# A gated pooling and matrix-memory block on one core: row mathematics in turns, folded mixer maps, pooled columns gated and split in the input projection, matrix memory's rows loaded four chunks ahead

## The chip, the cores and the metric

The kernel runs on one core of a Trainium2 chip. The metric is the device time of one launch in microseconds, lower is better. A core has five engines that work side by side and meet through semaphores: TensorE (PE; its weight loads are listed as PEld), VectorE (DVE), ScalarE (ACT), GpSimd (POOL) and SyncE (SP), which in this kernel issues all DMA transfers from one queue.

## The reference, cut to what matters

The input is 2048 tokens of 1024 columns, float32. One projection makes all columns for two branches that are merged at the end:

```python
h = rms_norm(x, norm_pre_g)
u_a, z_a, q, k, v, o, z_b, gates, g_a, g_b = split(h @ w_in)

pooled = multiscale_pool(u_a)          # 4 groups of 256 columns, centred means over 2, 4, 8, 16 tokens, minus the token
mixed  = einsum('bsgc,gcd->bsgd', pooled, pool_mix_w)          # one 256 x 256 map for each group
y_a    = (mixed * pool_scale) * silu(z_a)

q, k = silu(centred_depthwise_conv(q, k))                      # 5 taps
h_fwd = mlstm_direction(q, k, v, i_pre[0], f_pre[0])           # 4 heads of 256, 16 chunks of 128 tokens
h_bwd = flip(mlstm_direction(flip(q), flip(k), flip(v), ...))
y_b = rms_norm_per_head(h_fwd + h_bwd) * mlstm_norm_g * sigmoid(o) * silu(z_b)

merged = sigmoid(g_a + b0) * (y_a @ w_proj_pool) + sigmoid(g_b + b1) * (y_b @ w_proj_mlstm)
out = x + rms_norm(merged @ w_out, norm_post_g)
```

In each direction of the matrix memory, a chunk adds its weighted keys and values to a 256 x 256 state, and its queries read the state and the other tokens of the chunk. The weights come from "row mathematics": for every direction, head and chunk, sums of the logarithms of the forget gates, running maxima, and exponentials of both.

## The kernel before

All products are made from float32 values split into a high and a low part ("hi" and "lo", type float32r): three matmuls (hi x hi, hi x lo, lo x hi) take the place of one (`mm3`, `acc3`). `split` makes the parts: ScalarE copies the high part, and VectorE or GpSimd subtracts it from the value. The state and score products of the matrix memory are plain float32.

**Input projection** (`phase1`). The tokens are done in two halves of 1024. The columns are done in 36 pairs of 128-column blocks (`in_pairs`). The first two pairs of each half are plain products (`quarters`). Each other pair is a Strassen product of seven parts, 12 matmuls of 128 x 128 by 512 each, in three pairs of PSUM banks A, B and C (`strassen`). `prep_w` makes the weight combinations in the first half and `keep_w` stores them to memory; in the second half `again_w` reads them back. The columns of a pair are finished by a function of its kind: `pair_qk` (convolution and SiLU), `pair_v` (transposes), `pair_u` (window sums, pooled columns to memory), `pair_z` (SiLU), `pair_o` and `pair_g` (gates). The function is a generator: its last part runs while the next pair's products are under way (`run(rest)`). Long tiles come from small pools with rotating buffers: "raw" three, "acc" four, "p" six, and one buffer "rb" in the pool `rows`.

With half 1, `row_math` does the row mathematics of all gates in the place before pair 6 in one piece (L515), with two round trips through memory ("ends", "carry"). `masked` then adds the triangular masks to the rows of each two chunks and stores them ("nm"), and the convolutions left over from the first half (`late_load`) use the "rb" buffer afterwards.

**Matrix memory** (`tail`, `mlstm`). For each head, `backward` makes the states of the backward direction one chunk at a time (`back0` loads keys and values, `back1` transposes and weighs keys, `back2` updates the state), sixteen chunks ahead of `front1` to `front3`, which do both directions of a chunk: scores, decay, the products, the forward state, the division. `load_rows` reads the masked rows (tile "negM", from "nm") and the scale rows ("isc") of two chunks, two chunks ahead. `finish` makes the output of four chunks and puts its store in a list that is issued after the step (L1310).

**Branch A** (`branch_a`) does the pooling branch's projection for 8 blocks of 256 tokens. `mixer` comes two blocks ahead of it: it loads pooled columns and SiLU gates, splits the pooled columns, multiplies them by the group's map (`mix_weights`, 48 matmuls in a block), applies scale and gate, and splits the result for `project`. **Branch B** (`branch_b`) projects the matrix memory's output and merges. **Output** (`output`) is a Strassen product again, with the norm and the residual.

The order of the instructions on each engine is made by the compiler's scheduler from the order of the program, with priorities (`high_priority`) and ties (`issue_after`) written in it.

Of the kernel before, what the change touches and what calls it, by code (L numbers as in the profile page):

```python
# [8 lines left out]
F32 = mybir.dt.float32  # L9
# [4 lines left out]
P = 128  # L14
# [23 lines left out]
LAP = 1  # L38
PB = 2
# [3 lines left out]
PX = "kT"  # L43
# [4 lines left out]
def in_pairs():  # L48
# [11 lines left out]
    light = [("v", 0), ("o", 0), ("z", 0), ("o", 1), ("v", 1), ("o", 2), ("z", 1), ("o", 3), ("v", 2), ("o", 4)]  # L60
    light += [("z", 2), ("o", 5), ("v", 3), ("o", 6), ("z", 3), ("o", 7)]
# [16 lines left out]
class Kernel:  # L78
# [21 lines left out]
    def mm3(self, ps, w, x, start, stop):  # L100

        nc = self.nc
        for kt in range(4):
# [4 lines left out]
            nc.tensor.matmul(ps, wl, xh, start=False, stop=stop and kt == 3, skip_group_check=True)  # L108


    def constants(self):
        nc, a = self.nc, self.a
        c = self.ctx.enter_context(self.tc.tile_pool(name="const", bufs=1))
        self.cpool = c
        load = self.load
        self.gpre = load("norm_pre_g", [P, KT])
        self.ident = load("ident", [P, P])
        self.halo_qk = c.tile([P, 16, 4], F32, tag="halo_qk", name="halo_qk")
        self.halo_u = c.tile([P, 8, 16], F32, tag="halo_u", name="halo_u")
        self.half_c = c.tile([P, 1], F32, tag="half_c", name="half_c")  # L120
# [4 lines left out]
        self.icnt = {}  # L125
        for w in WINDOWS:
# [10 lines left out]
    def load(self, name, shape):  # L137
        t = self.cpool.tile(shape, F32, tag=name, name=name)
        self.nc.sync.dma_start(t, self.a[name])
        return t  # L140
# [72 lines left out]
    def operands(self, half, H, hp, wc, pool, psum):  # L213
# [47 lines left out]
        if half == 0:  # L261
            with tc.high_priority():
                last = sums(0)
            self.cw = self.load("conv_w", [P, 16, TAPS])
            self.cb = self.load("conv_b", [P, 16])
            self.bm = self.load("b_merge", [P, 2, KT])
# [37 lines left out]
    def load_w(self, wr, i, kts):  # L304
        raw = wr.tile([P, 4, 2 * P], F32, tag="wraw", name=self.nm("wraw"))
        self.nc.sync.dma_start(raw, self.a["w_in"][i, :, kts, :])
        return raw

    def again_w(self, W, i, wr, wc):

        nc, w_in = self.nc, self.a["w_in"]
# [9 lines left out]
        nc.sync.dma_start(left, w_in[i, :, :, :P])  # L321
# [11 lines left out]
        self.read = nc.sync.dma_start(b22, w_in[i, :, 4:8, P:])  # L333
# [35 lines left out]
    def strassen(self, H, W, psum, pool, out, n=BLK, swap=False):  # L369
# [13 lines left out]
        def prod(k, h, w, start):  # L383
            x, y = (H[h], W[w]) if not swap else (W[w], H[h])
            self.mm3(bank[k], y, x, start, True)
# [12 lines left out]
        prod("B", "S3", "T3", False)  # L398
# [38 lines left out]
    def phase1(self):  # L437
        tc, nc, a = self.tc, self.nc, self.a
        with ExitStack() as es:
            hp = {  # L440
# [18 lines left out]
            wg = None  # L459
            n = len(self.pairs)  # L460
            late, waits = [(kind, h) for h in range(NH) for kind in "qk"], None
            for half in range(2):
# [49 lines left out]
                rest = iter(())  # L512
# [1059 lines left out]
```

## Time and profile before

| what | us |
|---|---|
| median of 3 runs | 2386.11 |
| lowest and highest | 2384.36, 2393.65 |
| the profiled execution | 2388.18 |
| its span, first to last instruction | 2386.4 |
| mean granted TensorE clock | 0.993 of full |

The stages follow each other in the span. By TensorE's work: the first half of the input projection until about 739 us, the second until about 1456, the matrix memory until about 1790, branch A until about 2031, branch B until about 2213, then the output.

The span is one execution on the chip as the hardware profiler recorded it. A line of groups gives source line, engine, operation, tiles written and read, shape, count, then busy time and mean duration in ns, and then the idle time of the engine ahead of these instructions with what ended it. A tile view gives shortest, median and longest duration, and the start of the first and the last instruction. A windows view gives, for each stretch, its length and then busy time and instruction count of each engine, the granted clock and the DMA load. The chain of waits is followed back from the last instruction, so a transfer or an engine in it is what the rest stood for. Matmuls are pipelined: durations of neighbours overlap, and a busy share says less than how many start in a microsecond.

### The profile page before, as it was taken

To read this page: it belongs to the slowest core of one execution; us is meant where nothing else is said; L and a number is where in the kernel's file an instruction comes from. 1 tells how busy PE (TensorE), PEld (TensorE's weight loads), DVE (VectorE), ACT (ScalarE), POOL (GpSimd) and SP (SyncE) were. 2 spreads that over 40 slices of the span, in tenths; PEclk is the share of its full clock that TensorE was granted. 3 is DMA by queue.
4 is the path that set the end of the run, shared out by engine and by line. 5 is a ranking of instruction groups with operands and counts; after the bars stand their busy time and mean duration, and the time that the engine had idled before them with its cause. 6 is when DMAs were issued, how large, how long until landed. Compare 5 with 4: busy or idle time off the path is not lost.

```text
span 2386.4 us, 35771 instructions
## 1 busy us (share of the span) xinstructions
PE 2313.3 (97%) x12569; PEld 1998.1 (84%) x12569; DVE 1468.2 (62%) x2495; ACT 898.2 (38%) x1773; POOL 1139.3 (48%) x902
## 2 busy tenths in 40 slices
PE   7899999999999989999999999998999999999998
PEld 5688888888887878888888887997989899999776
DVE  6876676677666465565666434887875333354765
ACT  5435333333334333323322234766764112120442
POOL 4655564555544434464564540554555111233775
PEclk9999999999999999999999999999999999999999
DMA  4467656566673566787787867766657546588763
GB/s 151 175 225 273 234 194 238 203 230 215 233 260 135 166 192 216 260 282 256 246 272 239 269 221 253 231 214 208 197 161 230 176 146 208 183 283 280 249 215 124
DMA packets 303011, 521.63 MB, mean 219 GB/s; under 512 B 27504, under 2 KB 138224, under 8 KB 302832
## 3 DMA queue, kind: packets, MB, share of 16 engines
q1 hardware_dynamic: 302832, 519.35, 65.3%
q8 instruction: 99, 1.62, 0.3%
q14 instruction: 80, 0.66, 0.1%
HBM read 318.45 MB, written 200.80 MB: 218 GB/s over the span
## 4 chain that ended last, share of the span: by engine, by line
PE 79%; DVE 8%; DMA 7%; issue 2%; POOL 2%; ACT 2%; SPq 1%; DVEq 0%; POOLq 0%; ACTq 0%
PE bankB L106 8%; PE bankB L107 8%; PE bankB L108 8%; PE bankA L108 5%; PE bankA L107 5%; PE bankC L107 5%; PE bankA L106 5%; PE bankC L106 5%; PE bankC L108 5%; PE num L1212 3%; PE pb L921 2%; PE pb L922 2%; PE pb L920 2%; PE paps L921 2%; PE paps L922 2%
## 5 line engine op out<-in xcount | busy, mean ns | idle before, releaser
L98 POOL TENSOR_TENSOR wB21l<-wraw,wB21h 128x512 fp32r<-128x512 f32 x76 | 107.6, 1416 | 218.9 <-ACT wB21h L94 178.8
L627 DVE SCALAR_TENSOR_TENSOR acc<-raw,conv_w,acc 128x1026 f32<-128x1026 f32 (+1 forms) x96 | 155.8, 1636 | 10.6 <-ACT acc L622 9.7
L1196 POOL TENSOR_TENSOR qs<-q,isc 128x256 f32<-128x256 f32 x120 | 91.6, 766 | 145.3 <-PE num L1212 63.4
L98 POOL TENSOR_TENSOR wB22l<-wraw,wB22h 128x512 fp32r<-128x512 f32 x76 | 116.6, 1535 | 77.8 <-ACT wB22h L94 55.8
L922 PE MATMUL pb<-oxs,w_proj_mlstml 128*128 128x256 f32 x512 | 143.8, 281 | 0.0
L921 PE MATMUL pb<-oxs,w_proj_mlstmh 128*128 128x256 f32 x512 | 143.8, 281 | 0.0
L920 PE MATMUL pb<-oxs,w_proj_mlstmh 128*128 128x256 f32 x512 | 143.5, 280 | 0.0
L921 PE MATMUL paps<-pys,w_proj_poolh 128*128 128x256 f32 x512 | 142.6, 281 | 0.2 <-POOL pys L98 0.2
L920 PE MATMUL paps<-pys,w_proj_poolh 128*128 128x256 f32 x512 | 141.6, 281 | 1.2 <-DVE sga L1049 1.2
L922 PE MATMUL paps<-pys,w_proj_pooll 128*128 128x256 f32 x512 | 141.3, 281 | 0.0
L98 POOL TENSOR_TENSOR wB11l<-wraw,wB11h 128x512 fp32r<-128x512 f32 x72 | 108.9, 1513 | 54.4 <-ACT wB11h L94 53.6
L395 DVE TENSOR_TENSOR u<-bankB,p 128x512 f32<-128x512 f32 x76 | 52.2, 687 | 107.8 <-PE bankB L108 95.1
L106 PE MATMUL bankC<-S1h,wT1h 128*128 128x512 f32 x272 | 106.5, 392 | 3.4 <-ACT sg L738 3.4
L106 PE MATMUL bankB<-S3h,wT3h 128*128 128x512 f32 x272 | 106.3, 391 | 2.3 <-DVE u L395 2.3
L108 PE MATMUL bankB<-S2h,wT2l 128*128 128x512 f32 x272 | 106.3, 391 | 1.2 <-DVE wT2l L98 1.2
L106 PE MATMUL bankA<-A12h,wB21h 128*128 128x512 f32 x272 | 106.8, 393 | 0.5 <-ACT p L389 0.5
L107 PE MATMUL bankB<-S2l,wT2h 128*128 128x512 f32 x272 | 107.0, 393 | 0.0
L106 PE MATMUL bankB<-A22h,wT4h 128*128 128x512 f32 x272 | 105.9, 389 | 0.8 <-DVE u L400 0.8
L108 PE MATMUL bankC<-S1h,wT1l 128*128 128x512 f32 x272 | 106.5, 392 | 0.0
L107 PE MATMUL bankC<-S1l,wT1h 128*128 128x512 f32 x272 | 106.4, 391 | 0.0
L106 PE MATMUL bankB<-S2h,wT2h 128*128 128x512 f32 x272 | 106.2, 391 | 0.0
L107 PE MATMUL bankB<-S3l,wT3h 128*128 128x512 f32 x272 | 106.0, 390 | 0.0
(443 smaller groups left out, 7677.9 us busy)
## 6 DMA issues: line engine op xcount, KB each, us to landing
wraw<-in_w_in SPq DMA_DIRECT2D x110, 512.0 KB, 4.4
wt<-wT2h SPq DMA_DIRECT2D x34, 256.0 KB, 3.8
wt<-wT1h SPq DMA_DIRECT2D x34, 256.0 KB, 4.6
wt<-wT3h SPq DMA_DIRECT2D x34, 256.0 KB, 3.8
wt<-wT2l SPq DMA_DIRECT2D x34, 256.0 KB, 4.8
wt<-wT1l SPq DMA_DIRECT2D x34, 256.0 KB, 4.3
wt<-wT3l SPq DMA_DIRECT2D x34, 256.0 KB, 3.1
wt<-wT4h SPq DMA_DIRECT2D x34, 256.0 KB, 2.0
```

The source lines that it names most:

```text
L98: return eng.tensor_tensor(lo, x, hi.bitcast(F32), op=ALU.subtract)
L106: nc.tensor.matmul(ps, wh, xh, start=start and kt == 0, stop=False, skip_group_check=True)
L107: nc.tensor.matmul(ps, wh, xl, start=False, stop=False, skip_group_check=True)
L108: nc.tensor.matmul(ps, wl, xh, start=False, stop=stop and kt == 3, skip_group_check=True)
L395: self.read_banks.append(nc.vector.tensor_tensor(u2, bank["B"], p1, op=ALU.add))
L627: nc.vector.scalar_tensor_tensor(acc[:, :n], raw[:, tap : tap + n], self.cw[:, ct, tap : tap + 1], acc[:, :n], op0=ALU.mult, op1=ALU.add,)
L920: nc.tensor.matmul(ps, wh, xh, start=i == 0, stop=False)
L921: nc.tensor.matmul(ps, wh, xl, start=False, stop=False)
L922: nc.tensor.matmul(ps, wl, xh, start=False, stop=i == n)
L1196: nc.gpsimd.tensor_tensor(qs[d], q[:, :, ck], isc[:, d, j % 2, None, :].to_broadcast([P, 2, P]), op=ALU.mult)
L1212: nc.tensor.matmul(pn, qs[d][:, kt, :], state[:, kt, :], start=kt == 0, stop=False)
```

## The change

- **Row mathematics in turns.** `row_math` becomes a generator with six parts, one each in the places of pairs 3, 4, 6, 7, 9 and 10 of the second half. Each part but the last ends after it has issued DMAs whose results the next part reads. The leftover convolutions begin at pair 10 in place of 7.
- **Mixer's maps folded.** Pooling works on tokens and the map on columns, so the map can be applied to the input weights first. A new generator `fold` multiplies each group's 1024 x 256 block of `w_in` by its map times the scale, in float32, and stores it ("wu"). It runs in eight steps in the first half, with a load part in the place of one pair and a product part in that of the next. The pairs "u" read these weights.
- **Pooled columns gated and split in the input projection.** `pair_u` reads the SiLU gates of its columns, multiplies, splits, and stores both parts ("ya"). The pairs "z" move ahead of the "u" of the same group. `mixer` and `mix_weights` are gone; `pooled` in their place loads the two parts. The weight tiles of branch A that are loaded inside the matrix memory are more by the rooms that the maps took.
- **Matrix memory's rows loaded four chunks ahead**, with three buffers in place of two for the masked rows. Keys are read one chunk earlier than values, and gates in the fourth chunk of a group in place of the second.
- Tiles that only the projection needs go to a pool `first`, which is given back after it.

```diff
+FOLDS = (3, 5, 7, 9, 12, 14, 16, 18)
+ROWS = (3, 4, 6, 7, 9, 10)
...
+    def fold(self, pool, psum):
+        nc, a, tc = self.nc, self.a, self.tc
+        for g in range(4):
+            for half in range(2):
+                room = self.rows.tile([P, HALF], F32, tag="rb", name=self.nm("fm"))
+                m, sc = room[:, : 2 * DH].rearrange("p (c n) -> p c n", c=2), room[:, 2 * DH : 3 * DH]
+                nc.sync.dma_start(m, a["pool_mix_w"][g])
+                nc.sync.dma_start(sc, a["pool_scale"][g * DH : (g + 1) * DH].partition_broadcast(P))
+                w = pool.tile([P, 2, 4 * P], F32, tag="acc", name=self.nm("fw"))
+                nc.sync.dma_start(w, a["w_uT"][g, :, :, half * 4 * P : (half + 1) * 4 * P])
+                yield
+                nc.gpsimd.tensor_tensor(m, m, sc[:, None, :].to_broadcast([P, 2, DH]), op=ALU.mult)
+                for k2 in range(2):
+                    ps = psum.tile([P, 2, DH], F32, tag="tr", name=self.nm("fps"), bufs=2)
+                    for k in range(2):
+                        n0 = (k2 * 2 + k) * P
+                        with tc.issue_after(self.third.ins):
+                            for ct in range(2):
+                                nc.tensor.matmul(
+                                    ps[:, k, :], w[:, ct, n0 : n0 + P], m[:, ct, :], start=ct == 0, stop=ct == 1
+                                )
+                    o = pool.tile([P, 2, DH], F32, tag="p", name=self.nm("fo"))
+                    nc.scalar.activation(o, ps, AF.Copy)
+                    kt = half * 4 + k2 * 2
+                    nc.sync.dma_start(self.sp[f"wu{g}"][:, kt : kt + 2, :], o)
+                yield
...
-                    if half == 1 and i == 6:
-                        self.row_math(psum)
+                    if half == 1 and i in ROWS:
+                        with tc.issue_after(self.read.ins):
+                            next(rowmath, None)
...
-            nc.sync.dma_start(self.sp[f"pooled{g}"][:, i, tstart : tstart + n], d[:, :n])
+            z = pool.tile([P, HALF + 24], F32, tag="acc", name=self.nm("zu"))
+            nc.sync.dma_start(z[:, :n], self.sp[f"zs{g}"][:, i, tstart : tstart + n])
+            nc.vector.tensor_tensor(d[:, :n], d[:, :n], z[:, :n], op=ALU.mult)
+            nc.scalar.activation(z[:, :n].bitcast(F32R), d[:, :n], AF.Copy)
+            nc.gpsimd.tensor_tensor(d[:, :n].bitcast(F32R), d[:, :n], z[:, :n], op=ALU.subtract)
+            for p, y in enumerate((z, d)):
+                nc.sync.dma_start(self.sp[f"ya{g}"][:, p, i, tstart : tstart + n], y[:, :n])
...
-    def mixer(self, t, mix, ya):
+    def pooled(self, t, ya):
         for g in range(4):
             ys = ya[t, g] = self.pair_of("v1h" if g < 2 else "v1l", "pys")
+            for p in range(2):
+                self.nc.sync.dma_start(ys[:, p].bitcast(F32), self.sp[f"ya{g}"][:, p, :, t * TT : (t + 1) * TT])
...
-                nm = io.tile([P, 2, 2, P], F32, tag="negM", name=self.nm("negM"), bufs=SB)
+                nm = io.tile([P, 2, 2, P], F32, tag="negM", name=self.nm("negM"), bufs=SI)
...
-                if j % 2 == 0 and at + 2 < NH * NC_:
-                    load_rows((at + 2) // NC_, (at + 2) % NC_)
-                if j == 1:
+                if j % 2 == 0 and at + 4 < NH * NC_:
+                    load_rows((at + 4) // NC_, (at + 4) % NC_)
+                if j == 3:
                     load_gates(h, g)
...
             def aside():
-                mix.extend(self.mix_weights(raws, w1))
-                WA.update(self.weights("w_proj_pool", 0, range(2), raws, w1))
+                WA.update(self.weights("w_proj_pool", 0, range(6), raws, w1))
...
-            self.mixer(1, mix, ya)
-            WA.update(self.weights("w_proj_pool", 0, range(6, 8), raws, w2))
-            WA.update(self.weights("w_proj_pool", 1, range(8), raws, w2))
+            self.pooled(1, ya)
+            WA.update(self.weights("w_proj_pool", 1, range(2, 8), raws, w2))
```

More of the change, by code (lines that the diff above doesn't have):

```diff
@@ L125, in constants @@
         self.icnt = {}
+        c = self.first
         for w in WINDOWS:
@@ L135, in constants, with load @@
             self.icnt[w] = (lo, hi)
-    def load(self, name, shape):
-        t = self.cpool.tile(shape, F32, tag=name, name=name)
+    def load(self, name, shape, pool=None):
+        t = (pool or self.cpool).tile(shape, F32, tag=name, name=name)
         self.nc.sync.dma_start(t, self.a[name])
@@ L439, in phase1 @@
         with ExitStack() as es:
+            self.first = es.enter_context(tc.tile_pool(name="first", bufs=1, side="right"))
+            self.constants()
             hp = {
@@ L511, in phase1 @@
                 run(ops)
[L512 removed]
+                rest, fold = iter(()), self.fold(pool, psum)
                 for i in range(2, n):
[L514 to L515 removed]
+                    if half == 1 and i == 8:
                         mask = self.decay.tile([P, 2, P], F32, tag="mask", name="mask", bufs=1)
@@ L540, in phase1 @@
                     run(rest)
+                    if half == 0 and i in FOLDS:
+                        next(fold)
                     next(this)
                     rest = this
+                    if half == 0 and i + 1 in FOLDS:
+                        next(fold)
                     if half == 1 and waits is not None and i >= 7 and self.pairs[i][0] not in "qkuv":
@@ L546, in phase1 @@
                         waits = None
-                    elif half == 1 and waits is None and late and i >= 7:
+                    elif half == 1 and waits is None and late and i >= 10:
                         with tc.issue_after(self.read.ins):
@@ L770, in spills @@
                 sp[f"v{p}{h}"] = self.dram(f"v{p}{h}", [P, NC_, DH + 2])
-            for k in ("pooled", "zs", "sga", "sgb"):
+            sp[f"wu{h}"] = self.dram(f"wu{h}", [P, KT, 2 * P])
+            sp[f"ya{h}"] = self.dram(f"ya{h}", [P, 2, 2, S])
+            for k in ("zs", "sga", "sgb"):
                 sp[f"{k}{h}"] = self.dram(f"{k}{h}", [P, 2, S])
@@ L968, in out_weights @@
             self.split(*o, made[n], "act", "pool" if k % 2 else "dve")
-    def mix_weights(self, raws, pool):
-        nc = self.nc
-        out = []
-        for g in range(4):
-            raw = raws.tile([P, 2, DH], F32, tag="wraw", name=self.nm("mraw"))
-            nc.sync.dma_start(raw, self.a["pool_mix_w"][g])
-            out.append(tuple(pool.tile([P, 2, DH], F32R, tag="w", name=self.nm(f"mx{p}")) for p in "hl"))
-            self.split(*out[g], raw, "act", "dve")
-        return out
     def wt(self, W, kt, n0, n=P):
@@ L1052, in branch_a @@
                 if d == 1 and t + 2 < n:
-                    self.mixer(t + 2, mix, ya)
+                    self.pooled(t + 2, ya)
     def mlstm(self, aside=None, then=None, last=None):
```

119 lines of the change are left out of this document (58 added, 61 removed).

## The prediction

> **What bounds the kernel now.** I read the page first: the busy shares and the shares of the chain that ended last.
>
> ```profile
> PE 2313.3 (97%) x12569; PEld 1998.1 (84%) x12569; DVE 1468.2 (62%) x2495; ACT 898.2 (38%) x1773; POOL 1139.3 (48%) x902
> PE 79%; DVE 8%; DMA 7%; issue 2%; POOL 2%; ACT 2%; SPq 1%; DVEq 0%; POOLq 0%; ACTq 0%
> ```
>
> TensorE sets the time, and the 21% of the chain that is not TensorE shows where it runs dry. "Busy" hides part of that, because the matmuls overlap. So I counted instructions by stretch: the count after the second number (TensorE's) against that of a full neighbour.
>
> ```profile
> core 0: us, PE busy (x) PEld busy (x) DVE busy (x) ACT busy (x) POOL busy (x), PEclk, DMA share, GB/s
> 480.00:540.00 60.00, 59.81 (x272) 49.45 (x271) 46.28 (x57) 20.34 (x35) 33.17 (x23) 1.00 0.67 234
> 840.00:870.00 30.00, 23.67 (x105) 19.11 (x104) 12.09 (x35) 7.44 (x13) 7.08 (x6) 0.94 0.57 125
> 900.00:930.00 30.00, 30.00 (x135) 24.82 (x134) 8.71 (x16) 7.24 (x12) 5.18 (x4) 1.00 0.71 240
> 1500.00:1560.00 60.00, 60.00 (x429) 56.99 (x428) 54.50 (x182) 42.12 (x127) 30.66 (x41) 1.00 0.67 208
> 1600.00:1650.00 50.00, 41.37 (x262) 37.24 (x260) 36.16 (x122) 31.49 (x90) 21.05 (x27) 0.93 0.74 234
> 1740.00:1790.00 50.00, 44.27 (x277) 40.19 (x276) 37.58 (x131) 31.75 (x92) 28.96 (x36) 0.97 0.60 175
> ```
>
> At 840 to 870, 30 of 135 instructions are missing: 30 / 4.5 per us = 6.7 us lost. At 1500 to 1560 the matrix memory runs at 7.15 per us; 1600 to 1650 lacks 358 - 262 = 96, or 13.4 us, and 1740 to 1790 lacks about 80, or 11 us (a rough figure, since the mix of matmuls changes there). The input projection elsewhere is full (480 to 540).
>
> **The change part by part.**
>
> **1. The mixer leaves the tail.** The tile views of its matmuls (first and last of three lines) and of the second branch's projection (likewise):
>
> ```profile
> L920 PE MATMUL mps<-pxs,mxh x128: 276/281/390, 1790.6 to 1985.1; 128*128 128x256 f32 x128
> L922 PE MATMUL mps<-pxs,mxl x128: 276/280/289, 1790.9 to 1985.3; 128*128 128x256 f32 x128
> L920 PE MATMUL pb<-oxs,w_proj_mlstmh x512: 276/280/288, 2031.5 to 2212.5; 128*128 128x256 f32 x171
> L922 PE MATMUL pb<-oxs,w_proj_mlstml x512: 276/281/286, 2031.8 to 2212.8; 128*128 128x256 f32 x171
> ```
>
> The 280 ns are latency, not cost: 3 x 512 matmuls of branch B take 2212.8 - 2031.5 = 181.3 us, 118 ns each. Branch A has as many, and from the first mixer matmul to the first of branch B are 2031.5 - 1790.6 = 240.9. The difference, 59.6 us, is 3 x 128 mixer matmuls x 118 ns = 45.3 and 14.3 of stalls. What ends those stalls stands in the chain:
>
> ```profile
> 1803.59 3.60 DMA xz<-pooled
> ...
> 1824.48 6.51 DMA wraw<-in_w_proj_pool
> ...
> 1860.12 4.65 DMA pa<-sga
> ```
>
> The loads of pooled columns, their splits and the shared buffers go with the mixer; two reads per group and step remain, as many bytes as before and two steps ahead. Late next are the weights: six chunks (second half of the columns) are still loaded when the matrix memory ends, four load rooms are there, and they cover 96 matmuls x 118 ns = 11.3 us. First split, one more load (6.5 us) and the last splits take about as long: a stall between 0 and 8 us, taken as 3. **Term: -59.6 + 3 = -56.6.**
>
> **2. Matrix memory's rows.** The chain in 1600 to 1680, what SyncE's queue issued before the first of these waits, and what that queue itself waited for:
>
> ```profile
> 1603.87 7.39 DMA negM<-nm
> ...
> 1626.55 8.26 DMA negM<-nm
> ...
> 1639.97 2.86 DMA wraw<-in_w_proj_pool
> ...
> 1668.21 9.28 DMA negM<-nm
> ```
> ```profile
> 1600.42 1.94 SPq L1152 DMA_DIRECT2D gb<-gB  x2
> 1602.46 0.66 SPq L1114 DMA_DIRECT2D v<-vl  x1
> ...
> 1603.87 1.57 SPq L1156 DMA_DIRECT2D negM<-nm  x2
> ```
> ```profile
> SPq L1160 <- POOL qs L1196: 49.1, 20, 6.5
> SPq L1156 <- ACT dm L1188: 20.3, 13, 3.9
> ```
>
> ```profile
> L1185 PE MATMUL s<-q,kT x256: 270/275/582, 1486.0 to 1790.5; 128*128 128x128 f32 x128
> ```
>
> The masked rows come behind gates and values in one queue, and wait for one of two buffers. The 64 chunks take 304.5 us by their score products, 4.76 each: four chunks are 19 us instead of 9.5 for two, and a third buffer makes them usable; that covers the 7.4 to 9.3 us. The inter-chunk scale rows keep three buffers, so their place in the queue moves but not the buffer they wait for; behind that wait stand keys, values, queries, gates and the stored results, all needed two chunks later or more. The keys' read one chunk earlier and the gates' two later move no work. I take 8 of the 13.4 us, 1 for the wait at 1668, and 3 of the 11 at the end, where the mixer's splits of its first columns disappear but the splits of four chunks of weights stay: **-12** (bounds 0 and -24).
>
> **3. Row mathematics in turns.** Chain at 840 to 870:
>
> ```profile
> 844.54 9.51 DMA ends<-rows
> 854.12 5.00 DMA rows<-ends
> ...
> 861.66 1.97 PE vtr L653 x8
> ```
>
> VectorE sat behind a row operation that waited for two round trips through memory, with the split of transposed values behind it and TensorE behind that. In turns, each trip has a pair or more (7 products x 12 matmuls x 30 / 135 = 19 us) to land. The operations are the same; constants that move to other memory cost nothing. The late convolutions start three pairs later, and eight slots remain for eight. **-6** (bounds 0, -6.7).
>
> **4. The folds.** Eight steps x 2 x 2 x 2 = 64 products of full float32, 256 columns. The nearest rows are the state products, 258 columns, float32:
>
> ```profile
> 1734.97 0.87 PE num L1212 x4
> ```
> ```profile
> L1212 PE MATMUL num<-cf,qs 128*128 128x258 f32 x240 | 66.1, 385 | 0.0
> ```
>
> 60 chunks x 2 products gave 240 instructions, so each is two, of 0.87 / 4 = 218 ns. 64 x 2 x 218 ns = **+27.8 us**, in a stretch where TensorE is full, so all of it on the path. The GpSimd product ahead of each step and 16 ScalarE copies lie beside it (those engines are 48% and 38% busy), and so do eight times four reads and two stores; were TensorE to wait for the GpSimd product (1.4 us like the splits, by the group below), 8 x 1.4 = 11 more. I take 0: the loads come a whole pair earlier.
>
> **5. Pooled columns gated and split.** Sixteen tiles gain a load, a VectorE product, a ScalarE copy, a GpSimd difference and a second store. The nearest rows of about 1024 elements, and a split:
>
> ```profile
> L684 DVE TENSOR_TENSOR win<-win x24: 1204/1542/2331, 349.5 to 1295.1; 128x1016 f32<-128x1016 f32 x6, 128x1032 f32<-128x1032 f32 x6, 128x1020 f32<-128x1020 f32 x2, 128x1028 f32<-128x1028 f32 x2
> L632 POOL TENSOR_TENSOR acc<-acc,raw 128x1026 f32<-128x1026 f32 x16 | 41.3, 2578 | 16.5 <-ACT raw L631 16.3
> L631 ACT ACTIVATE raw<-acc 128x1026 f32<-128x1026 f32 x16 | 17.0, 1065 | 34.7 <-DVE acc L627 34.7
> L98 POOL TENSOR_TENSOR wT1l<-wt,wT1h 128x512 fp32r<-128x512 f32 x34 | 47.2, 1387 | 93.9 <-ACT wT1h L94 79.9 <-DVE pooled L688 5.4 <-DVE p L704 4.8
> ```
>
> VectorE gets 16 x 1.54 = 25 us, GpSimd 16 x 2.58 = 41, against the 1486 us before the first score product: room on average, not where the windows are widest:
>
> ```profile
> 505.46 2.20 DVE win L684
> ...
> 1286.41 2.69 DMA pooled<-pooled
> 1289.11 1.94 POOL win L684
> ...
> 1300.53 0.50 PE bankB L106
> ```
>
> The chain runs through such tiles at two of the eight groups, near 505 and near 1286. There the next tile's first sum waited for a store to free its buffer, and TensorE for VectorE. The four buffers now serve one tile more, and before its store lie 1.54 + 1.07 + 2.58 = 5.2 us more. The new loads and stores are queued on SyncE ahead of weight reads; what they hold up there is read a pair, 19 us, ahead. A floor is 0 (TensorE's banks hide it; sigmoid columns no longer follow the widest group), a ceiling is four tiles (those of two groups, where the chain leaves TensorE) x (5.2 + 2.7) = 32. I take the products alone, 4 x 1.54 = **+6**, because TensorE at 480 to 540 lost almost nothing with such a chain.
>
> A rule that speaks against this: the Trainium skill, "SBUF — State Buffer", section "Who interferes with whom", says that a VectorE operation with two SBUF inputs and a GpSimd operation that reads SBUF shut each other out for a whole instruction. The spread above (1204 to 2331 ns for one shape class) agrees that such operations are sometimes lengthened, without showing by whom. By the rows alone this part costs 6 us; by that rule it is the third rival below.
>
> **The sum.** -56.6 - 12 - 6 + 27.8 + 6 = -40.8. The profiled run took 2388.18 us (span 2386.4 and 1.8 around it), 2.1 above the median of the three runs; the difference applied to that median, 2386.1, gives **2345 us**.
>
> **The rivals.**
> - **More is recovered:** the matrix memory gets all 24, the pooled tiles hide: -56.6 - 24 - 6.7 + 27.8 = -59.5, 2327 us. For it: every stall named is a wait, not work. Against: VectorE is busy 54.5 of 60 there. 12%.
> - **The rows are a cover:** another load takes their place (weights at 1639.97, the scale rows' 49.1 us of queue waits), and the matrix memory gains nothing: 2357. Against: the masked rows' wait is the longest piece of each gap. 18%.
> - **VectorE and GpSimd in each other's way at the pooled tiles.** The 16 differences hold up VectorE for their length, 2.58 us; at the tiles of the two widest groups of each half, eight, it reaches TensorE, 20.6 us, and half of the 11 at the folds, where a GpSimd product and VectorE's weight differences meet, 5.5: 2371. For it: the spread of 1204 to 2331 ns. Against: VectorE is 62% busy. 14%. (It is what the page of the Trainium skill on SBUF, cited in part 5, would make of this change.)
> - **Slower: the four buffers of the pooled tiles.** If the next window sum waits for the split's store at all 16 tiles, in VectorE's order with evacuations behind it, each costs up to 7.9 us (5.2 + 2.7). Without my 6 the sum is -46.8, so it decides from 46.8 / 16 = 2.9 us per tile that reach TensorE; at half of 7.9 it is 63 - 46.8 = +16, 2402 us. Against: so far only two of eight groups let a chain through. 6%.
> - **No gain at all as described** cannot be for part 1: the matmuls are gone from the stage.
>
> **How the numbers follow.** Forecast 50%, the rivals as given (12, 18, 14, 6). Half a per cent (12 us) is about what a measurement can tell from no change: 2374 and 2398 bound "same". Faster: 50 + 12 + 18 + 6 of the 14 = 86%; same: the other 8; slower 6. The range 2325 to 2373 leaves out the slow case, half of the third and a little at the lower end: under 20%.
>
> **What would show each step.** Right: branch A 182 to 188 us with no mixer matmuls; 128 new matmul instructions of about 218 ns in the first half, which grows by 28 to 36 us; no gap at 840 to 870 and no wait on masked rows in the chain; a matrix memory stage 10 to 15 us shorter. Wrong: TensorE waits on VectorE after each pooled group (part 5); the fold's products waiting for GpSimd (part 4); the first projection of branch A waiting for weights for over 8 us (part 1).

## The result, and the profile after

The changed kernel is slower by half a per cent: a median of 2399.17 us in seven runs, against 2386.11 in seven of the kernel before beside them; the ratio is 1.0054 (95% interval 1.0044 to 1.0064). The forecast was 2345 us, with a range of 2325 to 2373. The profiled execution has a span of 2397.5 us, 11.1 more than before.

The page of the changed kernel, busy shares (its chain of waits reaches back only over the output stage, so the stages are read from tile and windows views):

```profile
PE 2308.5 (96%) x12313; PEld 1986.5 (83%) x12313; DVE 1453.8 (61%) x2411; ACT 881.0 (37%) x1737; POOL 1157.4 (48%) x894
```

TensorE issues 256 matmul instructions fewer (384 of the mixer gone, 128 of the folds new) and yet the span grew. The tile views of the folds, the scores and both branches (columns as before):

```profile
L337 PE MATMUL fps<-fm,fw x128: 377/379/454, 122.4 to 448.9; 128*128 128x256 f32 x128
...
L1221 PE MATMUL s<-q,kT x256: 270/275/582, 1555.4 to 1855.3; 128*128 128x128 f32 x128
...
L978 PE MATMUL paps<-pys,w_proj_poolh x512: 274/281/582, 1839.6 to 2041.1; 128*128 128x256 f32 x171
...
L978 PE MATMUL pb<-oxs,w_proj_mlstmh x512: 274/281/356, 2041.4 to 2222.9; 128*128 128x256 f32 x171
```

From such first and last starts comes a table by stage. "Half 1" ends here with the last product of tile A11h with B11h in the second half's first pair (758.8 before, 805.3 after), "half 2" with the first score, "matrix memory" with the last score, "branch A" with the first projection of branch B. The first of these ends, in the kernel before and in the changed one:

```profile
L426 PE MATMUL bankA<-A11h,wB11h x8: 389/390/393, 739.6 to 758.8; 128*128 128x512 f32 x8
```
```profile
L463 PE MATMUL bankA<-A11h,wB11h x8: 389/389/389, 786.2 to 805.3; 128*128 128x512 f32 x8
```

| us | before | after | difference |
|---|---|---|---|
| half 1 | 758.8 | 805.3 | +46.5 |
| half 2 | 727.2 | 750.1 | +22.9 |
| matrix memory | 304.5 | 299.9 | -4.6 |
| branch A | 241.0 | 186.1 | -54.9 |
| branch B, output, end | 354.9 | 356.1 | +1.2 |

So branch A gave what was forecast, and the input projection took more than all of it. The windows view of the changed kernel shows where; a full 20 us hold 90 instructions in the projection (4.5 per us) and about 143 in the matrix memory:

```profile
core 0: us, PE busy (x) PEld busy (x) DVE busy (x) ACT busy (x) POOL busy (x), PEclk, DMA share, GB/s
360.00:380.00 20.00, 18.89 (x85) 15.50 (x84) 11.44 (x15) 5.10 (x9) 10.39 (x8) 1.00 0.76 270
380.00:400.00 20.00, 16.69 (x68) 13.35 (x67) 19.24 (x20) 6.06 (x10) 13.92 (x8) 0.91 0.60 203
640.00:660.00 20.00, 16.32 (x65) 13.08 (x65) 15.83 (x14) 6.78 (x11) 11.53 (x8) 0.88 0.62 212
900.00:920.00 20.00, 15.21 (x63) 12.43 (x62) 8.89 (x20) 5.08 (x7) 2.08 (x2) 0.83 0.78 242
1100.00:1120.00 20.00, 17.69 (x71) 14.15 (x71) 14.57 (x15) 4.84 (x9) 12.80 (x9) 0.91 0.82 264
1360.00:1380.00 20.00, 18.46 (x74) 15.16 (x75) 16.54 (x19) 6.86 (x11) 12.89 (x7) 0.91 0.76 258
1400.00:1420.00 20.00, 16.92 (x67) 13.29 (x66) 9.37 (x10) 6.90 (x11) 12.85 (x7) 0.91 0.72 235
...
1695.40:1715.40 20.00, 15.04 (x93) 13.91 (x92) 12.50 (x41) 13.50 (x37) 8.76 (x11) 0.83 0.82 279
1815.40:1835.40 20.00, 18.77 (x112) 16.77 (x111) 16.73 (x51) 12.53 (x36) 13.81 (x16) 0.91 0.91 299
```

Six of the seven projection stretches lack 16 to 27 instructions, 3.6 to 6 us each, and run at a lower granted clock (the one at 900 to 920 is the gap before the transposed values, treated below). One such place from near, in the timeline of the changed kernel (start, duration, engine, line; in brackets the idle time before it and what ended it):

```profile
379.24 1.22 DVE L734 SCALAR_TENSOR_TENSOR pooled<-win,raw 128x1016 f32<-128x1016 f32 x1
...
387.97 2.74 POOL L745 TENSOR_TENSOR pooled<-pooled,zu 128x1016 fp32r<-128x1016 f32 x1
...
388.44 3.35 DVE L734 SCALAR_TENSOR_TENSOR pooled<-win,raw 128x1016 f32<-128x1016 f32 x1
391.70 0.68 DVE L757 TENSOR_TENSOR u<-bankC,u 128x512 f32<-128x512 f32 x1
```
```profile
392.44 0.80 PE L107 MATMUL bankC<-S4h,wB22h 128*128 128x512 f32 x1 [3.31 <-DVE u L757]
```

TensorE waits 3.31 us for a bank that VectorE empties at 391.70. VectorE is not idle: a pooled column that took 1.22 us one tile earlier takes 3.35 beside GpSimd's new difference, and the evacuation (the copy of a bank's result out of it) stands behind it. Ahead of another gap of TensorE, 3.68 us up to 656.59, VectorE had waited too, for a weight split that GpSimd had queued behind the new difference (the timeline again):

```profile
635.10 2.92 POOL L745 TENSOR_TENSOR pooled<-pooled,zu 128x1016 fp32r<-128x1016 f32 x1
...
640.47 1.29 POOL L99 TENSOR_TENSOR wT1l<-wt,wT1h 128x512 fp32r<-128x512 f32 x1
...
641.80 1.75 DVE L389 TENSOR_TENSOR wt<-wraw,wt 128x512 f32<-128x512 f32 x1 [5.42 <-POOL wT1l L99]
```

Between this wait and the gap lie 11 us of other work of VectorE, so that the wait caused the gap is likely and not shown.

And the gap before the transposed values, near 860 us before, is still there; VectorE ahead of it:

```profile
901.96 0.07 DVE L693 MEMSET vnl<- 128x8 f32 x1 [6.82 <-DMA qT<-acc]
902.92 0.18 DVE L916 TENSOR_TENSOR_SCAN rows<-rows 4x16 f32<-4x16 f32 x1 [0.90 <-DMA rows<-ends]
```

The long wait is for one of the four shared "acc" buffers, which a convolution's store still holds. The row mathematics waits behind it for 0.9 us, and once more for 1.26 us at 905.15. The kernel before had the same wait at the same operation, a longer one:

```profile
859.00 0.07 DVE L647 MEMSET vnl<- 128x8 f32 x1 [9.38 <-DMA qT<-acc]
```

### The profile page after: what moved, and what is told of

Same layout as the page of the kernel before. It is cut to its first block, busy times and chain, and to the rows that moved or that the text cites. A ratio compares the mean times of both kernels' runs of the same rounds, so it can differ in the third digit from the quotient of the medians.

```text
span 2397.5 us, 35173 instructions
## 1 busy us (share of the span) xinstructions
PE 2308.5 (96%) x12313; PEld 1986.5 (83%) x12313; DVE 1453.8 (61%) x2411; ACT 881.0 (37%) x1737; POOL 1157.4 (48%) x894
## 5 line engine op out<-in xcount | busy, mean ns | idle before, releaser
L978 PE MATMUL paps<-pys,w_proj_poolh 128*128 128x256 f32 x512 | 145.1, 284 | 5.0 <-DMA pys<-ya 2.6
L979 PE MATMUL paps<-pys,w_proj_poolh 128*128 128x256 f32 x512 | 144.6, 284 | 0.0
L107 PE MATMUL bankC<-S4h,wB22h 128*128 128x512 f32 x272 | 106.7, 392 | 3.3 <-DVE u L757 3.3
L109 PE MATMUL bankB<-A22h,wT4l 128*128 128x512 f32 x272 | 108.2, 398 | 0.0
L963 POOL TENSOR_TENSOR nm<-nm,mask 128x256 f32<-128x256 f32 x64 | 65.1, 1030 | 89.0 <-DMA nm<-negM 88.8
L108 PE MATMUL bankB<-A22l,wT4h 128*128 128x512 f32 x272 | 108.0, 397 | 0.0
```

Source lines behind the costliest of these rows:

```text
L107: nc.tensor.matmul(ps, wh, xh, start=start and kt == 0, stop=False, skip_group_check=True)
L108: nc.tensor.matmul(ps, wh, xl, start=False, stop=False, skip_group_check=True)
L109: end = nc.tensor.matmul(ps, wl, xh, start=False, stop=stop and kt == 3, skip_group_check=True)
L963: nc.gpsimd.tensor_tensor(t[:, d, :, :], t[:, d, :, :], mask[:, d, None, :].to_broadcast([P, 2, P]), op=ALU.add)
L978: nc.tensor.matmul(ps, wh, xh, start=i == 0, stop=False)
L979: nc.tensor.matmul(ps, wh, xl, start=False, stop=False)
```

## The experiments

Each kernel was timed against the kernel before on the same chip. The changed kernel is 1.0054 of it, 2396 to 2398 us in these comparisons. Ratios have their 95% intervals; differences of whole times below are worked out from them. Stage times come from the tile views, cut as in the table above, and each is from one execution. How far one scatters is seen where kernels have the same code in a stage: 182.5 to 186.1 us in branch A (the changed kernel, e1, e10, e19), 746.1 to 750.1 in half 2 (the changed kernel, e1, e10), 1512.4 to 1516.7 in both halves together (e2, e9, e17, e18). A stage difference under some 4 us can't be told from that.

| run | ratio to before | half 1 | half 2 | matrix memory | branch A |
|---|---|---|---|---|---|
| after | 1.0054 | 805.3 | 750.1 | 299.9 | 186.1 |
| e1_no_fold | 0.9907 (0.9892 to 0.9922) | 773.1 | 746.1 | 301.1 | 182.5 |
| e2_gate_tail | 0.9984 (0.9974 to 0.9993) | 791.1 | 725.6 | 325.7 | 184.5 |
| e3_split_tail | 1.0022 (1.0012 to 1.0031) | 793.3 | 735.6 | 318.7 | 184.5 |
| e4_low_dve | 1.0032 (1.0022 to 1.0043) | 802.3 | 746.5 | 297.0 | 185.8 |
| e9_gate_late | 0.9984 (0.9970 to 0.9997) | 788.1 | 724.3 | 325.5 | 182.2 |
| e10_rows2 | 1.0102 (1.0087 to 1.0117) | 805.6 | 747.3 | 316.3 | 184.8 |
| e13_rows_once | 0.9976 (0.9964 to 0.9988) | 788.5 | 721.9 | 325.1 | 182.5 |
| e14_acc5 | 0.9975 (0.9964 to 0.9987) | 787.4 | 729.3 | 321.6 | 184.0 |
| e17_tied | 0.9918 (0.9904 to 0.9933) | 787.4 | 726.1 | 298.8 | 193.3 |
| e18_tied_spread | 0.9928 (0.9910 to 0.9947) | 790.7 | 724.9 | 304.0 | 195.6 |
| e19_after_acc5 | 0.9983 (0.9973 to 0.9993) | 799.3 | 739.9 | 300.4 | 182.5 |
| e20_tied_acc5_rows | 0.9889 (0.9874 to 0.9904) | 784.8 | 721.7 | 301.9 | 192.5 |
| e21_acc5_low_dve | 0.9959 (0.9943 to 0.9975) | 798.1 | 738.8 | 297.8 | 183.6 |
| e22_earlier_start | 0.9886 (0.9869 to 0.9902) | 783.1 | 723.3 | 300.4 | 189.0 |

**The folds: e1_no_fold.** `columns` returns the input weights, and `fold` isn't called.

```diff
-        return self.sp[f"wu{g}"] if kind == "u" else self.a["w_in"][i]
+        return self.a["w_in"][i]
```

> Leaves out the folding of the maps: the pair of columns read the input weights as they are, so the mixer's maps are missing from the result. Theory A (the folds cost their 128 matmul instructions of 218 ns and nothing beside them): 28 us shorter than the changed kernel, 2371 us, and the gaps of TensorE near 392 and 656 us stay. Theory B (the GpSimd product and the reads and stores of the folds also hold up the weight splits): 35 to 45 us shorter, 2355 to 2364, and the first half of the projection ends within 5 us of the kernel before's 739.6.

Measured: 2361.4 us, 35 shorter. Half 1 lost 32.2 us, which is the 28 of the products and 4 more; half 2 and branch A, which have no fold, lost 4 and 3.6 beside it. These fours are no more than the scatter. By the whole time it lies where B begins, but half 1 is still 14 us longer than before, which B excludes. Of the two gaps that A kept, one stays and one is shorter, in TensorE's timeline of e1:

```profile
369.03 0.50 PE L107 MATMUL bankC<-S4h,wB22h 128*128 128x512 f32 x1 [1.05 <-DVE u L753]
...
625.28 0.50 PE L107 MATMUL bankB<-A22h,wT4h 128*128 128x512 f32 x1 [3.85 <-DVE u L437]
```

So the folds cost their matmuls and at most little beside them, and the rest of the growth is elsewhere.

**The pooled tiles: e2_gate_tail, e3_split_tail, e4_low_dve.** e2 stores the ungated column once and gates and splits in branch A; e3 keeps the gate and moves the split alone; e4 makes the difference on VectorE.

```diff
 # e2: pair_u (e3 keeps the z tile, its load and the product)
-            z = pool.tile([P, HALF + 24], F32, tag="acc", name=self.nm("zu"))
-            nc.sync.dma_start(z[:, :n], self.sp[f"zs{g}"][:, i, tstart : tstart + n])
-            nc.vector.tensor_tensor(d[:, :n], d[:, :n], z[:, :n], op=ALU.mult)
-            nc.scalar.activation(z[:, :n].bitcast(F32R), d[:, :n], AF.Copy)
-            nc.gpsimd.tensor_tensor(d[:, :n].bitcast(F32R), d[:, :n], z[:, :n], op=ALU.subtract)
-            for p, y in enumerate((z, d)):
-                nc.sync.dma_start(self.sp[f"ya{g}"][:, p, i, tstart : tstart + n], y[:, :n])
+            nc.sync.dma_start(self.sp[f"ya{g}"][:, 0, i, tstart : tstart + n], d[:, :n])
 # e2: pooled
+            xz = self.pair_of("kT", "xz", F32)
+            self.nc.sync.dma_start(xz[:, 0], self.sp[f"ya{g}"][:, 0, :, cut])
+            self.nc.sync.dma_start(xz[:, 1], self.sp[f"zs{g}"][:, :, cut])
+            self.nc.vector.tensor_tensor(xz[:, 0], xz[:, 0], xz[:, 1], op=ALU.mult)
+            self.split(ys[:, 0], ys[:, 1], xz[:, 0], "act", "pool")
 # e4
-            nc.gpsimd.tensor_tensor(d[:, :n].bitcast(F32R), d[:, :n], z[:, :n], op=ALU.subtract)
+            nc.vector.tensor_tensor(d[:, :n].bitcast(F32R), d[:, :n], z[:, :n], op=ALU.subtract)
```

> The pooled columns are stored once and ungated in the projection; gate and split move to the first branch (load of columns and gates, VectorE product, ScalarE copy, GpSimd difference per pair of groups). Theory A (the sixteen gated and split tiles cause TensorE's gaps in the projection, some 35 us in both halves): 30 to 38 us shorter than the changed kernel, 2361 to 2369 us, if the first branch takes it beside its matmuls; its 186 us may grow by up to 10. Rival (the new order of the pairs and the row mathematics in turns cause the gaps): projection unchanged within 8 us, 2392 to 2410 us.

> Load of the gates and VectorE product stay in the projection, the ScalarE copy, the GpSimd difference and the second store leave it; the split is made in the first branch. Theory A1 (GpSimd's sixteen differences, by the delayed weight splits behind them and by the lengthened VectorE operations beside them, are most of the loss): 20 to 30 us shorter than the changed kernel, 2370 to 2380 us. Theory A2 (the loads of gates and the VectorE products in the four shared buffers are the loss): under 8 us shorter, above 2391.

> The sixteen differences run on VectorE instead of GpSimd; nothing else moves. Theory A1 (GpSimd at the tiles): 8 to 20 us shorter than the changed kernel, 2380 to 2391 us, and the window sums of three pieces near 1354 us fall from 1.9 us to about 1.5 us each. Theory A2 (VectorE's queue at the widest groups is what TensorE waits for, whoever lengthens it): 5 to 25 us longer, since 16 operations of 1.3 us join that queue.

Measured: e2 took 14.2 us off half 1 and 24.5 off half 2, 38.7 together, as theory A had it (39 to 43 by the four kernels with this projection): with e1's 32.2 that is 70.9, and the projection had grown by 69.4. The rival falls, since e2 keeps the new order of the pairs and the turns. The windows view of e2 at places where the changed kernel lacked instructions:

```profile
380.00:400.00 20.00, 20.00 (x91) 16.68 (x90) 13.07 (x19) 7.34 (x13) 10.46 (x8) 1.00 0.69 236
640.00:660.00 20.00, 20.00 (x90) 16.57 (x89) 14.69 (x15) 7.68 (x13) 13.19 (x9) 1.00 0.57 200
880.00:900.00 20.00, 15.81 (x70) 12.72 (x69) 6.73 (x20) 4.63 (x8) 2.65 (x3) 0.91 0.89 244
1360.00:1380.00 20.00, 20.00 (x90) 16.47 (x89) 9.34 (x10) 5.36 (x8) 12.87 (x9) 1.00 0.69 235
```

They are full, but for the gap before the transposed values, now in 880 to 900. The two stretches of the pooled tiles as a whole, first of the changed kernel and then of e2:

```profile
340.00:660.00 320.00, 309.50 (x1364) 255.00 (x1363) 229.70 (x260) 114.07 (x190) 190.32 (x115) 0.99 0.67 236
1080.00:1420.00 340.00, 325.04 (x1415) 266.85 (x1415) 219.44 (x240) 104.05 (x151) 199.77 (x126) 0.98 0.79 266
```
```profile
340.00:660.00 320.00, 319.81 (x1430) 265.41 (x1429) 221.46 (x261) 112.36 (x188) 177.96 (x114) 1.00 0.63 222
1080.00:1420.00 340.00, 339.95 (x1516) 281.42 (x1515) 201.20 (x242) 104.03 (x151) 183.06 (x128) 1.00 0.78 259
```

The changed kernel has 167 instructions fewer there, 37 us at 4.5 per us. TensorE is idle for 25 of them, and the lower granted clock makes some 10 (0.01 x 320 + 0.02 x 340). End to end the time fell by only 17 us, though, since the matrix memory grew by 26; branch A, where the 10 were looked for, did not. e3 gave 26.5 of the 38.7 in the projection, so the split with its second store is the larger share and the gate's load and product the other 12; end to end its 7 us fell in A2's range, but by the stages that is A1 and a matrix memory longer by 19. e4 gave 6.6 in the projection and 5 in all, less than the 8 to 20 of its theory A1: GpSimd's differences count, but are the small part. The window sums and columns beside them, of which A1 expected sums of about 1.5 us, by the groups of lines with shapes kept apart (busy, mean ns), first the changed kernel and then e4:

```profile
L734 DVE SCALAR_TENSOR_TENSOR pooled<-win,raw 128x1016 f32<-128x1016 f32 x8 | 13.9, 1741 | 0.1
...
L730 DVE TENSOR_TENSOR win<-win 128x1032 f32<-128x1032 f32 x6 | 11.0, 1832 | 0.1
```
```profile
L734 DVE SCALAR_TENSOR_TENSOR pooled<-win,raw 128x1016 f32<-128x1016 f32 x8 | 11.8, 1472 | 0.1
...
L730 DVE TENSOR_TENSOR win<-win 128x1032 f32<-128x1032 f32 x6 | 9.0, 1496 | 1.2 <-POOL win L730 1.1
```

Without GpSimd's differences the same operations are 0.27 and 0.34 us shorter. The first row would mislead by itself, since it was longer still in the kernel before:

```profile
L688 DVE SCALAR_TENSOR_TENSOR pooled<-win,raw 128x1016 f32<-128x1016 f32 x8 | 14.9, 1858 | 0.1
```

The durations of all VectorE operations on these tiles that both kernels have add up to 82 us before, 94 in the changed kernel and 82 in e4, so the lengthening is real; it is 12 us beside 22 us of the new products.

**The buffers of the pooled tiles: e19_after_acc5, e21_acc5_low_dve.** The changed kernel with a fifth "acc" buffer, for which one product buffer ("p") and one weight buffer ("wc") are given up; e21 adds e4's edit.

```diff
-                        shape, dt, tag=tag, name=name, bufs=bufs or dict(p=6, acc=4).get(tag, 3)
+                        shape, dt, tag=tag, name=name, bufs=bufs or dict(p=5, acc=5).get(tag, 3)
-            wc = es.enter_context(tc.tile_pool(name="wc", bufs=20))
+            wc = es.enter_context(tc.tile_pool(name="wc", bufs=19))
```

> The changed kernel with five shared buffers for convolutions and pooled columns instead of four, five product buffers instead of six and 19 weight buffers instead of 20. Theory B (the pooled tiles' loss is that a tile now holds two buffers through a load, a product, a split and two stores, and the next window sum waits): the projection 15 to 30 us shorter, 2368 to 2382 us. Theory W (it is the added work in VectorE's queue itself): within 6 us of the changed kernel.

> The changed kernel with five shared buffers (as e19_after_acc5) and the sixteen differences on VectorE (as e4_low_dve). If the buffers and GpSimd's differences are two causes: 6 to 8 us shorter than e19_after_acc5, 2372 to 2375 us. If they are the same waits seen twice (the difference mattered because it held a buffer longer): within 3 us of e19_after_acc5. If VectorE's own added work is now what TensorE waits for: 3 to 10 us longer than e19_after_acc5.

Measured: e19 is 17 us shorter, 16.2 of them in the projection (theory B). It is the pooled tiles that need the buffer: the same fifth buffer in a kernel that stores them once and ungated (e14 against e9, below) gave nothing. The view of waits, first the changed kernel and then e19 (who waited for what: us, times, longest), shows one way in which a buffer counts: the gates' load can't start before "zu" has one.

```profile
DVE pooled L743 <- DMA zu<-zs: 16.8, 7, 7.1
```
```profile
DVE pooled L743 <- DMA zu<-zs: 4.6, 4, 3.6
```

e21 is 2.3 us shorter than e19 in the projection, where 6.6 would be the sum, but 6 us shorter end to end (intervals that overlap a little), where the sum would be 5. So whether the difference cost time by itself or because it kept a buffer longer stays open: the two readings lie about 4 us apart, as much as the scatter. Lengthened operations are no measure of the loss: in e19 the operations counted above add up to 98 us, more than in the changed kernel. Some 20 of the 38.7 us are left with both edits. Only e2 removes them; whether VectorE's product or the traffic of loads and stores holds them wasn't told apart.

**What e2 gave back: e9_gate_late, e17_tied.** e9 splits the tail's `pooled` into loads and, later in the program, products (`gated`); e17 ties the products with `issue_after` to a VectorE instruction of the chunk, or of the projection, beside which they stand. It also puts the first step's loads three chunks earlier in the program.

```diff
 # e17 against e9
-                    last(n)
+                    with tc.issue_after(cur["dm"].ins):
+                        last(n)
...
-                    self.gated(t + 1, ya, (d - 4,))
+                    with self.tc.issue_after(read.ins):
+                        self.gated(t + 1, ya, (d - 4,))
```

> As e2_gate_tail, but in the tail the columns and gates of a step are loaded a step's part ahead of the VectorE product that reads them (first step: loads two chunks before the end of the matrix memory, products in the last two chunks; later steps: loads at the second projection, products at the last four). Theory (the 26 us that e2_gate_tail gave back in the matrix memory are VectorE waiting for the loads of columns and gates, 7.7 us at the longest, with the state updates queued behind): matrix memory back from 325.7 to 300 to 304 us by the score products, projection as in e2_gate_tail, 2353 to 2361 us. Rival (the work itself, products and splits, does not fit beside the matrix memory): 2370 us or more.

> As e9_gate_late, but the products of the first branch's steps are tied behind a VectorE instruction of the chunk or projection beside which they stand in the program, so that the planner can't put them in VectorE's queue dozens of us earlier, in front of loads that haven't landed. Theory (the matrix memory's 26 us are those waits): 298 to 304 us by the score products, gaps near 1741, 1789 and 1806 gone, 2350 to 2360 us. Rival (work or memory traffic that doesn't fit there): 315 us or more, above 2368.

Measured: e9 changed nothing, 325.5 us for the matrix memory, and by its time it lies where its rival put it. Its timeline shows why; VectorE and then TensorE:

```profile
1740.03 0.69 DVE L1055 TENSOR_TENSOR xz<-xz 128x512 f32<-128x512 f32 x1 [5.43 <-DMA xz<-zs]
```
```profile
1741.17 0.58 PE L971 MATMUL cu<-v,k 128*128 128x258 f32 x1 [4.49 <-DVE cb L1120]
```

In the program this product stands in the last two chunks, later than 1820 us; the scheduler put it 80 us and more ahead, where its load had only been issued. Tied, the product runs 59 us later and waits for nothing, the stage is 298.8 and the rival falls:

```profile
1798.61 0.68 DVE L1055 TENSOR_TENSOR xz<-xz 128x512 f32<-128x512 f32 x1
```

The loads' new place is not the reason, as the first of them starts at 1727 us in both kernels. The whole is 32 us below the changed kernel, at 2365; the forecast of 2350 to 2360 missed by 5, since branch A starts with gaps and takes 193.3 us, 11 more than in e9.

**The gap before the transposed values: e13_rows_once, e14_acc5, e20_tied_acc5_rows.** e13 is e9 with the row mathematics in one piece ahead of pair 6. e14 is e9 with the fifth buffer. e20 is e17 with the fifth buffer and `ROWS = (3, 4, 7, 8, 9, 10)`, which puts the third and the fourth turn a pair later.

> e9_gate_late with the row mathematics in one piece ahead of the seventh pair, as before. Theory S (TensorE's gap near the first transposed values of the second half is VectorE's wait for a shared buffer that a convolution's store still holds, and has nothing to do with the row mathematics): within 3 us of e9_gate_late. Rival R (the round trips of the row mathematics stop TensorE, as the prediction had it): 5 to 8 us longer, with a second gap after the seventh pair's start.

> e9_gate_late with five instead of four of the shared buffers of convolutions and pooled columns, paid for by five instead of six product buffers and 19 instead of 20 weight buffers. Theory S: the gap of about 4 us before the transposed values near 890 us, with the lower clock behind it, is gone, 4 to 7 us shorter than e9_gate_late unless the missing buffers cost as much elsewhere. Rival R: the gap stays.

> e17_tied with five of the shared buffers as in e14_acc5, and the third turn of the row mathematics a pair later. Theory (two waits lie on top of each other at the gap before the transposed values near 890 us: the buffer, and the round trip of the row ends, 8.2 us in e14_acc5; only without both does it go): that gap under 1 us, 3 to 7 us shorter than e17_tied, less what the missing buffers cost. Rival: the gap stays.

Measured: e13 is within 3.4 us of e9, intervals overlapping, with no second gap; the turns alone are worth nothing here. They hardly spread the work, as the changed kernel's timeline shows (SyncE's queue, the loads of the first part; the scan of the fourth stands above, at 902.92):

```profile
856.92 4.98 SPq L871 DMA_DIRECT2D rows<-gates  x8
```

The places of these parts lie four pairs or 76 us apart, the instructions 46. e14 misses too: the gap is still 3.61 us. Its VectorE timeline tells the reason:

```profile
887.88 0.38 DVE L909 TENSOR_TENSOR_SCAN rows<-rows 4x16 f32<-4x16 f32 x2 [8.21 <-DMA rows<-ends]
```

With the buffer free, the same queue waits at the same place for the round trip of the row ends. Both waits lay on top of each other, and the one hid the other. Without both (e20), the stretch is full, in its windows view:

```profile
880.00:900.00 20.00, 20.00 (x94) 16.63 (x93) 11.47 (x16) 7.08 (x10) 4.96 (x3) 1.00 0.95 328
```

and e20 is at 2358.4 us, 7 below e17 (0.9889 against 0.9918, intervals just meeting). Of that, 4.4 us are in half 2, where the gap lay, and 2.6 in half 1, which has no such gap. The later turns alone, with four buffers, were not run.

**The rows: e10_rows2.** The earlier loading in the matrix memory undone in the changed kernel; the lines shown are a part of the edit, which also undoes the third buffer of the masked rows, the second load of rows at the start and the earlier read of the keys.

```diff
-                if j % 2 == 0 and at + 4 < NH * NC_:
-                    load_rows((at + 4) // NC_, (at + 4) % NC_)
-                if j == 3:
+                if j % 2 == 0 and at + 2 < NH * NC_:
+                    load_rows((at + 2) // NC_, (at + 2) % NC_)
+                if j == 1:
```

> The changed kernel with its second part undone: the masked rows and scale rows loaded two chunks ahead into two buffers, the gates at the second chunk of four, the keys' read not earlier. Theory (that part is worth what the stage lost, 4.6 us): matrix memory 303 to 306 us by the score products against 299.9, 2400 to 2404 us, that is 3 to 6 us above the changed kernel. Rival (the part does more, and the weights' splits in the middle of the stage hide it): 8 to 13 us above.

Measured: 11 us above the changed kernel by the ratios (12 by the profiled executions), 16.4 in the matrix memory (316.3). The theory falls, and the time lies in the rival's range; that the weights' splits hide the rest, as the rival says, isn't shown. The view of waits over that stage, of e10 and of the kernel before:

```profile
ACT dm L1223 <- DMA negM<-nm: 21.3, 5, 5.7
```
```profile
ACT dm L1188 <- DMA negM<-nm: 15.5, 5, 5.3
```

In the changed kernel no wait for the masked rows is left in that view. The part is worth 16 us there and 11 in the whole. But without it the stage would be 12 us longer than before; which of the other edits does that is open.

**The middle of the matrix memory, and the start of branch A: e18_tied_spread, e22_earlier_start.** e18 loads the six weight chunks in three places instead of one; e22 is e20 with one split of the first step in each of the last four chunks, its loads two chunks earlier, and the second step's splits two projections earlier.

> e17_tied with the six weight chunks that are loaded and split in the middle of the matrix memory spread over three places, two each, four chunks apart. Theory (the gap of 2 + 3 us in the middle, in the kernel before too, is those splits in the queues of VectorE and ScalarE): 4 to 8 us shorter than e17_tied. Rival (only the first pair of loads matters): the gap stays, within 2 us.

> e20_tied_acc5_rows with the first step's four gated splits one each in the last four chunks, and the second step's two projections earlier. Theory (the first branch starts late because its first operands are split late): first branch 184 to 188 us instead of 192.5, 2351 to 2356 us. Rival (the weights' splits at the same place are what it waits for): 190 us or more, within 3 us of e20_tied_acc5_rows.

Measured: e18 is no better (304.0, and 0.9928 against 0.9918). In its timeline a gap of 3.84 us remains, behind this split, so what counts there is not how many splits there are:

```profile
1699.52 0.69 DVE L99 TENSOR_TENSOR w_proj_pooll<-wraw,w_proj_poolh 128x512 fp32r<-128x512 f32 x1 [3.77 <-ACT w_proj_poolh L95]
```

e22 has 189.0 in branch A, half of what was looked for, and its time, 2356.5, can't be told from e20's. Both theories keep a part. e22 is the fastest kernel of the study: 0.9886 of the kernel before, 27 us below it and 40 below the changed one.

## Why the prediction was wrong

The terms as forecast and as the stages and runs have them:

| part | forecast | measured | from |
|---|---|---|---|
| 1 mixer leaves the tail | -56.6 | -54.9 | branch A |
| 2 rows | -12 | -4.6 (alone -16 in the stage, -11 in the whole) | matrix memory; e10 |
| 3 row mathematics in turns | -6 | 0 | the gap stays; e13 |
| 4 folds | +27.8 | +32 | half 1 of e1 |
| 5 pooled tiles | +6 | +39 (to 43) | both halves of e2 (e9, e17, e18) |

- **Part 5 is the step that failed.** It took "the products alone", +6, "because TensorE at 480 to 540 lost almost nothing with such a chain", and its ceiling counted only the four tiles of the two groups in the chain. In the changed kernel TensorE had ten gaps of 0.66 to 4.72 us from 392 to 656 and from 1095 to 1416 us that e2 hasn't; the pooled tiles lie from 340 to 638 and from 1086 to 1374. The chain had shown where VectorE was late before, and not how little was missing elsewhere. The measured 39 lie above the ceiling of 32.
- **The slow rival came nearest.** It let the next window sum wait for the split's store and put the limit at 2.9 us per tile; 38.7 / 16 = 2.4 us were lost. Its shared buffers were part of the cause, since a fifth gave 16 us back, but not by that wait: in the changed kernel's view of waits no window sum waits for a store. There the product waits for the gates (16.8 us), and other work for the pooled tiles' stores (3.4 us before a tile "vnh", 2.8 before an evacuation). The third rival (VectorE and GpSimd in each other's way, priced at 20.6 us, and 2371 us) was real, by the 94 us against 82 above, but is worth 5 to 7. The Trainium skill, "SBUF — State Buffer", section "Who interferes with whom", says that such a pair excludes each other for a whole instruction. The traces agree: the column of 3.35 us ends 1.08 us after GpSimd's difference does, and the column before it took 1.22 us in all. By e4 most of the loss lay elsewhere. So parts of two rivals held together, at 20% between them, where the forecast let only one hold at a time. What makes up the 20 us left with both edits is open.
- **Part 4** was right in its price: 128 instructions, as forecast. The 4 us beside them, no more than the scatter, had been set at nothing and at most 11.
- **Part 1** was right: 186.1 against 182 to 188 forecast.
- **Part 2** had the right mechanism, and its wait is gone. The measured 16 (11 in the whole) lie within its bounds. What failed is that the rest of the stage was taken as it was: 12 of the 16 were given back by something that isn't found.
- **Part 3 read the chain wrongly.** The chain's two rows, "ends<-rows" and "rows<-ends", are the store and the load of one round trip and not two trips, and the row that ended VectorE's wait was another, "qT<-acc" (9.38 us in the kernel before, 6.82 in the changed one). Both waits were there (e14, e20). To remove the buffer's wait alone gave nothing. Nor do the turns give each trip "a pair or more", 19 us: from the store of the ends (890.07 in SyncE's timeline of the changed kernel) to the scan that reads them (902.92) are 12.9 us.
- The stages add up to the whole: -54.9 - 4.6 + 69.4 + 1.2 = +11.1, where 69.4 is the projection, of which the folds (32) and the pooled tiles (39) explain all, within the scatter.

## What to carry to other kernels

An engine that is 62% busy can still have no room: what counts is the queue at the places where the tensor engine already waits for it, and how many rotating buffers the added step holds for how long. Work moved from a short stage into a long one should be tried with its buffers and its waits apart and together, since one wait can hide another at the same place. An instruction whose input comes by DMA needs a tie to the place where it is meant to run, as a place late in the program is no place late in the queue.

## What the runs showed of the hardware

- A gap of TensorE can cost more than it lasts. At 380 to 400 us, a gap of 3.31 us is 15 instructions at 4.5 per us, and 22 are missing, with a granted clock of 0.91: 0.09 of 20 us is 1.8 us, or 8 instructions more. At 360 to 380 a gap of 1.11 us costs the 5 instructions that it lasts, at 1.00. The Trainium skill, "TensorE: Matmul & The Clock Gate", section "What's actually happening", has the clock fall after an idle window of about 3.4 us. The changed kernel's trace agrees for the gaps of 3.31 us and more, but one of 3.08 us (1400 to 1420, 0.91) and one of 2.31 us (1100 to 1120, 0.91 and 19 missing) were enough as well.
- Small operations of VectorE are not small beside GpSimd. Edge columns of two elements, in the changed kernel's timeline, beside GpSimd's work and at the next tile without it:

```profile
380.49 1.72 DVE L738 TENSOR_TENSOR pooled<-win,il 128x2 f32<-128x2 f32 x1
...
392.31 0.15 DVE L738 TENSOR_TENSOR pooled<-win,il 128x2 f32<-128x2 f32 x1
```
